# Forget logits of a two-layer hybrid decoder: activations as the stationary operand instead of the weights

## The chip, the cores and the metric

One core of one Trainium2 chip runs the whole program. The metric is the device time of one execution in microseconds (us). Engines are named as in the profile: PE (matrix multiply), PEld (its weight loads), DVE (vector), ACT (scalar and activation), POOL, SP (issues DMAs).

## The reference, cut to what matters

Two layers on 256 tokens of width 1024. Each layer is a SwiGLU block, a mixer and a second SwiGLU block. The mixer projects the normalised activations `h` to queries, keys, values, forget logits (8 columns, one for each head) and the inputs of a recurrent branch. The forget logits enter the attention through a cumulative sum over tokens:

```
h = rms_norm(x, mix_norm[l])
proj = h @ w_in[l] + b_in[l]
q, k, v, f_logit, xr, gr, g_attn, g_rnn = jnp.split(proj, SPLIT_POINTS, axis=-1)
log_f = jax.nn.log_sigmoid(f_logit.astype(jnp.float32))
...
c = jnp.cumsum(log_f, axis=1).transpose(0, 2, 1)
s = jnp.einsum('bhqd,bhkd->bhqk', q_i, k).astype(jnp.float32) * scale
s = s + (c_i[..., :, None] - c[:, :, None, :])
```

## The kernel before, in words

Activations lie transposed: channels on the 128 partitions, in eight chunks, and the 256 tokens along the free axis. The tile `xs` holds for each chunk a rounded part `hi` (columns 0 to 255) and the rest `lo` (256 to 511), both in the type `fp32r`. Each weight block is loaded as `wr`, and split the same way by ACT (`CAST`, the high part) and DVE (`TENSOR_TENSOR`, the rest) into tiles `W` or `R`. A product is three matmuls: high by high, high by low, low by high. One matmul instruction of PE is recorded as a weight load (PEld) of its stationary operand, and a MATMUL over its moving operand. Rows of the order and of the profile name the operands as `out<-moving,stationary`: the forget matmul before the change is `B<-xs,wf`, with the shape `128*16 128x256` in the trace, that is 16 stationary columns and 256 moving ones. The tile `wf2` of the code stands there as `wf`.

The order of instructions on all engines is set while the program is built, by a planner. It keeps a model clock for each engine. The big matrix products are `steps`; everything else is a generator (`forget`, `stats`, `projected`, `qk`, `head`, ...), which yields a time or a condition until which it is put off. When a step is planned, the generators that are due are advanced first, and what they issue goes into the engines' queues there. Each queue is then worked off in this order on the chip, with semaphores between engines.

`mix` starts `forget` at eight steps after the first query projection. `stats` computes the reciprocal norm of each token (`rst`, tokens on partitions) and its copy along the free axis (`rb`); its second pair of matmuls is `B<-S,ones_r`. The weights of the forget logits, 8 columns for each chunk, are split into `wf2`: 8 high columns and 8 low ones side by side.

`forget` before the change: for each chunk, one matmul with the 16 columns of `wf2` stationary and the 256 tokens of `hi` moving, and one with the 8 high columns stationary and `lo` moving. They add up in one PSUM bank, with the 16 logit rows on partitions and tokens along the free axis. The bank is copied by ACT or DVE (`flex`) into the zeroed tile `fpad`, and two PE transposes turn that into tokens on partitions. From there on before and after agree: four small DVE operations make `f` (norm, bias, high plus low part), `log1pexp` makes the log of the sigmoid in about fifteen small DVE operations and an Exp on ACT, three matmuls with `tri` and `ones` make the cumulative sum, DVE copies it into `cpad`, PE transposes `cpad`, and a DMA through DRAM spreads it over the partitions (`cb`), which each `head` needs. In the first layer `decays` runs a second such chain on DVE (`tiny<-prm`, `sp`) behind the first.

Of the kernel before, what the change touches and what calls it, by code (L numbers as in the profile page):

```python
# [23 lines left out]
F32 = mybir.dt.float32  # L24
F32R = mybir.dt.float32r
AF = mybir.ActivationFunctionType
ALU = mybir.AluOpType
# [175 lines left out]
class Trunk:  # L203
# [346 lines left out]
    def setup(self):  # L550
        c = self.const
        self.cpad = c.tile([128, 128], F32, name="cpad")
        self.DVE.memset(self.cpad, 0.0)
        self.fpad = c.tile([128, 256], F32, name="fpad")
        self.POOL.memset(self.fpad, 0.0)
        self.prm_sb = c.tile([128, L, NP_], F32, name="prm")

        self.x0 = c.tile([128, 8 + 2048], F32, name="x")
        self.x = self.x0[:, 8:].rearrange("p (a b) -> p a b", a=8)
        cut = lambda k: slice(8 + 256 * k if k else 0, 264 + 256 * k)  # L560
        load_x = lambda q, k: q.dma_start(out=self.x0[:, cut(k)], in_=self.xT_in[:, cut(k)])
        for k in range(2):
            load_x(self.ACT, k)
        self.load_piece(0, slice(0, W0 // 2))
        self.load_piece(0, slice(W0 // 2, W0))
        self.load_piece(0, slice(W0, 2 * W0))
        for k in range(2, 8):
            load_x(self.SP, k)
            if k < 6:
                self.load_piece(k // 2, slice(k % 2 * W0, k % 2 * W0 + W0))  # L570
        self.ACT.activation(self.t([128, 1], "ss", 4), self.cpad[:, 0:1], AF.Silu)
        warm = self.take(self.banks)
        for _ in range(WARM):
            self.PE.matmul(warm[:, 0:128], self.cpad, self.cpad, start=True, stop=True)
        self.banks.give(warm)

        self.idents = c.tile([128, 256], F32, name="idents")
        self.ident = self.idents[:, 0:128]
        self.POOL.memset(self.idents, 1.0)
        self.POOL.affine_select(out=self.idents, in_=self.idents, compare_op=ALU.is_equal, fill=0.0, base=0,  # L580
                                pattern=[[0, 2], [-1, 128]], channel_multiplier=1)
        self.ones = c.tile([128, 128], F32, name="ones")
        self.POOL.memset(self.ones, 1.0)
        self.ones_r = self.t([128, 192], "ones_r", 1, F32R, self.ops)[:, 16:144]
        self.DVE.tensor_copy(self.ones_r, self.ones)
        self.mhalf = c.tile([128, 8], F32, name="mhalf")
        self.DVE.memset(self.mhalf, -0.5)
        self.xs = self.t([128, 8, 512], "xs", 1, F32R, self.ops)
        self.starts.append((16, self.load_parameters, "bias"))
        self.starts.append((30, self.constants, "bias"))  # L590
# [314 lines left out]


    def forget(self, M):
        pt = self.take(self.banks)
        for k in range(8):

            xs = self.x_rhs(M["phase"], k)
            self.PE.matmul(pt[0:16, 0:256], M["wf2"][:, k], xs[:, 0:256], start=k == 0, stop=False)
            self.PE.matmul(pt[0:8, 0:256], M["wf2"][:, k, 0:8], xs[:, 256:512], start=False, stop=k == 7)
        self.flex(self.fpad[0:16], pt[0:16, 0:256])
        self.banks.give(pt)
        yield self.when(self.fpad, must=lambda: M["phase"] in self.rb, bank=True, queues=())
        pt = self.take(self.banks)
        p3 = self.transpose(pt, self.fpad)
        f = self.t([128, 2, 8], "f", 1)
        for t in range(2):  # L920
            r = self.rms(M["phase"])[:, t:t + 1]
            self.DVE.scalar_tensor_tensor(f[:, t], p3[:, t, 8:16], r, M["bf"], op0=ALU.mult, op1=ALU.add)
            self.DVE.scalar_tensor_tensor(f[:, t], p3[:, t, 0:8], r, f[:, t], op0=ALU.mult, op1=ALU.add)
        self.banks.give(pt)
        yield self.when(f, queues=())
        lp = self.log1pexp(f, [128, 2, 8])
        self.DVE.tensor_scalar(f, f, 0.0, None, op0=ALU.min)
        self.DVE.tensor_sub(f, f, lp)
        if M["l"] == 0:
            self.decays()  # L930
        yield self.when(f, bank=True, queues=())
        pt = self.take(self.banks)
        mm = self.PE.matmul
        mm(pt[:, 0:8], self.tri, f[:, 0], start=True, stop=True)
        mm(pt[:, 8:16], self.ones, f[:, 0], start=True, stop=False)
        mm(pt[:, 8:16], self.tri, f[:, 1], start=False, stop=True)
        self.DVE.tensor_copy(self.cpad[:, 0:16], pt[:, 0:16])
        self.banks.give(pt)
        nc = self.t([128, 16], "nc", 2)
        self.DVE.tensor_scalar(nc, self.cpad[:, 0:16], -1.0, None, op0=ALU.mult)  # L940
        yield self.when(nc, bank=True, queues=())
        pt = self.take(self.banks)
        self.PE.transpose(pt[:, 0:128], self.cpad, self.ident)
        cT = self.t([16, 128], "cT", 1)
        self.DVE.tensor_copy(cT, pt[0:16, 0:128])
        self.banks.give(pt)
        cd = self.dram.tile([16, 128], F32, tag="cd", name="cd", bufs=2)
        yield self.when(cT, queues=())
        self.SP.dma_start(out=cd, in_=cT)
        yield self.when(cd, queues=())  # L950
        M["cb"] = [self.slot([8, 128]) for _ in range(2)]
        for t in range(2):
            self.SP.dma_start(out=M["cb"][t][0][:, 0:1024], in_=bass.AP(tensor=cd.tensor, offset=cd.offset + t * 1024,
                                                                          ap=[[0, 128], [1, 1024]]))
        M["nc"] = nc
# [356 lines left out]
```

## Time and profile before

| | |
|---|---|
| median of 3 runs | 1221.62 us (1221.45 to 1222.02) |
| the profiled execution | 1221.39 us, of which span 1219.7 us |
| PE busy | 1214.3 us, 100% of the span |
| PEld busy | 1187.3 us, 97% |
| DVE busy | 856.6 us, 70% |
| ACT busy | 701.3 us, 57% |
| POOL busy | 39.2 us, 3% |

A timeline row gives the start and length of a group of equal instructions in us, then engine, line, operation, tiles, shapes (for PE the stationary operand as partitions * columns, then the moving one), the count, and in brackets idle time ahead of it with what ended it. [...] All instructions have line 160, the helper that issues them.

### The profile page before, as it was taken

To read this page: it belongs to the slowest core of one execution; us is meant where nothing else is said; L and a number is where in the kernel's file an instruction comes from. 1 tells how busy PE (TensorE), PEld (TensorE's weight loads), DVE (VectorE), ACT (ScalarE), POOL (GpSimd) and SP (SyncE) were. 2 spreads that over 40 slices of the span, in tenths; PEclk is the share of its full clock that TensorE was granted. 3 is DMA by queue.
4 is the path that set the end of the run, shared out by engine and by line. 5 is a ranking of instruction groups with operands and counts; after the bars stand their busy time and mean duration, and the time that the engine had idled before them with its cause. 6 is when DMAs were issued, how large, how long until landed. Compare 5 with 4: busy or idle time off the path is not lost.

```text
span 1219.7 us, 24091 instructions
## 1 busy us (share of the span) xinstructions
PE 1214.3 (100%) x10024; PEld 1187.3 (97%) x10024; DVE 856.6 (70%) x1419; ACT 701.3 (57%) x1231; POOL 39.2 (3%) x48
## 2 busy tenths in 40 slices
PE   9999999999999999999999999999999999999998
PEld 9999998989999999999999999989899999999998
DVE  6775566886869877656677555677876698886742
ACT  6554455789685565444455444465887855654431
POOL 0000000101000000000000000011010000000000
PEclk9999999999999999999999999999999999999999
DMA  7575564543456565545556545646544455565551
GB/s 283 206 252 175 182 234 170 193 179 138 173 171 213 199 248 208 173 173 173 207 208 239 176 149 180 235 145 228 173 142 172 171 207 208 208 224 192 174 191 53
DMA packets 36894, 232.48 MB, mean 191 GB/s; under 512 B 4624, under 2 KB 7088, under 8 KB 10032
## 3 DMA queue, kind: packets, MB, share of 16 engines
q1 hardware_dynamic: 36496, 230.66, 53.8%
q8 instruction: 79, 1.29, 0.4%
q10 hardware_dynamic: 288, 0.27, 0.1%
q14 instruction: 31, 0.25, 0.1%
HBM read 229.85 MB, written 1.06 MB: 189 GB/s over the span
## 4 chain that ended last, share of the span: by engine, by line
PE 98%; ACT 1%; DVE 1%; DMA 0%; issue 0%; ACTq 0%
PE B L160 98%; DVE tiny L160 0%; ACT junk L160 0%; DMA x<-xT 0%; ACT W L160 0%; ACT L160 0%; DVE S L160 0%; ACT xs L160 0%; ACT tiny L160 0%; DVE x L160 0%; DVE sp L160 0%; DVE f L160 0%; DVE sp_neg L160 0%; DVE rq L160 0%; DVE rst L160 0%
## 5 line engine op out<-in xcount | busy, mean ns | idle before, releaser
L160 DVE TENSOR_TENSOR W<-wr,W 128x1024 fp32r<-128x1024 f32 (+2 forms) x316 | 380.3, 1209 | 155.7 <-ACT W L160 153.9
L160 PE MATMUL B<-xs,W 128*128 128x256 f32 x3984 | 472.7, 278 | 0.9 <-ACT W L160 0.9
L160 PEld LDWEIGHTS B<-xs,W 128*128 128x128 f32 x3984 | 462.2, 189 | 2.2 <-ACT W L160 1.2
L160 ACT CAST W<-wr 128x1024 fp32r<-128x1024 f32 (+2 forms) x316 | 323.7, 1034 | 162.5 <-PE B L160 136.4
L160 PE MATMUL B<-R,W 128*128 128x256 f32 x2520 | 291.6, 276 | 0.0
L160 PEld LDWEIGHTS B<-R,W 128*128 128x128 f32 x2520 | 288.3, 188 | 0.0
L160 PE MATMUL B<-xs,R 128*128 128x256 f32 x1776 | 207.5, 276 | 0.0
L160 PEld LDWEIGHTS B<-xs,R 128*128 128x128 f32 x1776 | 204.4, 188 | 0.2
L160 DVE TENSOR_TENSOR R<-wr,R 128x1024 fp32r<-128x1024 f32 x112 | 135.3, 1220 | 35.7 <-ACT R L160 35.7
L160 ACT ACTIVATE S<-S 128x256 f32<-128x256 f32 x88 | 36.1, 418 | 146.2 <-DVE S L160 146.2
L160 PE MATMUL B<-W,xs 128*128 128x512 f32 x492 | 119.2, 393 | 0.0
L160 ACT CAST R<-wr 128x1024 fp32r<-128x1024 f32 x112 | 114.6, 1042 | 0.9 <-DMA wr<-ws 0.9
L160 PEld LDWEIGHTS B<-W,xs 128*128 128x128 f32 x492 | 90.5, 188 | 17.9
L160 PE MATMUL B<-R,R 128*128 128x256 f32 (+1 forms) x808 | 102.8, 280 | 0.0
L160 PEld LDWEIGHTS B<-R,R 128*128 128x128 f32 x808 | 95.2, 188 | 0.0
L160 ACT ACTIVATE xs<-x,prm 128x256 fp32r<-128x256 f32 x40 | 20.1, 508 | 65.6 <-DVE x L160 65.6
L160 POOL TENSOR_TENSOR rst<-rst,mhalf 128x4 f32<-128x4 f32 (+1 forms) x22 | 28.6, 1305 | 888.2 <-DVE rst L160 868.4
L160 DVE TENSOR_TENSOR R<-S,R 128x256 fp32r<-128x256 f32 x88 | 36.5, 422 | 29.2 <-ACT R L160 29.2
L160 DVE TENSOR_TENSOR S<-B,S 128x256 f32<-128x256 f32 x88 | 36.5, 420 | 14.3 <-PE B L160 12.5
L160 ACT CAST R<-S 128x256 fp32r<-128x256 f32 x88 | 34.3, 398 | 13.6 <-DVE S L160 13.6
L160 DVE TENSOR_TENSOR sq<-B,rb 128x256 f32<-128x256 f32 x24 | 10.2, 425 | 43.6 <-PE B L160 43.6
L160 DVE TENSOR_TENSOR S<-B,rb 128x256 f32<-128x256 f32 x88 | 36.1, 418 | 0.1
(126 smaller groups left out, 677.3 us busy)
## 6 DMA issues: line engine op xcount, KB each, us to landing
wr<-ws SPq DMA_DIRECT2D x209, 1024.0 KB, 4.8
wr<-w SPq DMA_DIRECT2D x7, 384.0 KB, 5.4
bias<-b_in SPq DMA_DIRECT2D x8, 256.0 KB, 4.8
R<-wbd SPq DMA_DIRECT2D x4, 512.0 KB, 5.9
R<-cd SPq DMA_DIRECT2D x4, 512.0 KB, 5.9
out<-x SPq DMA_DIRECT2D x8, 128.0 KB, 1.7
x<-xT SPq DMA_DIRECT2D x6, 128.0 KB, 5.4
wr<-w SPq DMA_DIRECT2D x2, 192.0 KB, 3.7
```

Source lines behind the costliest of these rows:

```text
L160: return fn(*args, **kw)
```

## The change

The two operands of the forget matmuls are exchanged. For each half of the tokens (t = 0, 1) and each chunk, 128 tokens of `hi` are stationary and the 16 columns of `wf2` move, and 128 tokens of `lo` are stationary and its 8 high columns move. The result has tokens on partitions already: 16 columns of the bank for each t. `fpad`, its memset, its copy out of PSUM and the two transposes of it are gone, and DVE reads the bank itself. The matmuls are now issued only when `rb` of this phase has been planned, where the transposes were before.

```diff
     def forget(self, M):
+        yield self.when(must=lambda: M["phase"] in self.rb, bank=True, queues=())
         pt = self.take(self.banks)
-        for k in range(8):
-            xs = self.x_rhs(M["phase"], k)
-            self.PE.matmul(pt[0:16, 0:256], M["wf2"][:, k], xs[:, 0:256], start=k == 0, stop=False)
-            self.PE.matmul(pt[0:8, 0:256], M["wf2"][:, k, 0:8], xs[:, 256:512], start=False, stop=k == 7)
-        self.flex(self.fpad[0:16], pt[0:16, 0:256])
-        self.banks.give(pt)
-        yield self.when(self.fpad, must=lambda: M["phase"] in self.rb, bank=True, queues=())
-        pt = self.take(self.banks)
-        p3 = self.transpose(pt, self.fpad)
+        for t in range(2):
+            o, c = pt[:, t * 16:t * 16 + 16], slice(t * 128, (t + 1) * 128)
+            for k in range(8):
+                xs = self.x_rhs(M["phase"], k)
+                self.PE.matmul(o, xs[:, 0:256][:, c], M["wf2"][:, k], start=k == 0, stop=False)
+                self.PE.matmul(o[:, 0:8], xs[:, 256:512][:, c], M["wf2"][:, k, 0:8], start=False, stop=k == 7)
         f = self.t([128, 2, 8], "f", 1)
         for t in range(2):
             r = self.rms(M["phase"])[:, t:t + 1]
-            self.DVE.scalar_tensor_tensor(f[:, t], p3[:, t, 8:16], r, M["bf"], op0=ALU.mult, op1=ALU.add)
-            self.DVE.scalar_tensor_tensor(f[:, t], p3[:, t, 0:8], r, f[:, t], op0=ALU.mult, op1=ALU.add)
+            hi, lo = (pt[:, t * 16 + i:t * 16 + i + 8] for i in (0, 8))
+            self.DVE.scalar_tensor_tensor(f[:, t], hi, r, M["bf"], op0=ALU.mult, op1=ALU.add)
+            self.DVE.scalar_tensor_tensor(f[:, t], lo, r, f[:, t], op0=ALU.mult, op1=ALU.add)
```

Since the planner's clock moves with every instruction, the order around the change moves as well. On PE, in the first layer, this stands in the kernel before (the number behind `_` is a buffer; the last operand of a row is the stationary one; `128x512` matmuls belong to the query and key projections):

```order
L160 MATMUL B_2491<-xs,wf_2257 16x256
L160 MATMUL B_2491<-xs,wf_2257 8x256
L160 MATMUL B_2519<-R_2354,xs 128x512
...
L160 MATMUL B_2519<-W_2415,xs 128x512
L160 MATMUL B_2543<-S_2438,ones_r 128x256 x2
L160 MATMUL B_2554<-idents,fpad 128x128 x2
L160 MATMUL B_2530<-W_2415,xs 128x512
```

And this in the changed kernel, where 16 pairs like the two rows with `wf` follow each other:

```order
L160 MATMUL B_2506<-W_2413,xs 128x512
L160 MATMUL B_2533<-S_2436,ones_r 128x256 x2
L160 MATMUL B_2544<-wf_2255,xs 128x16
L160 MATMUL B_2544<-wf_2255,xs 128x8
...
L160 MATMUL B_2495<-R_2425,xs 128x512
```

The forget matmuls moved behind the second `ones_r` pair, and 32 stand where two transposes stood. Behind them, up to the three matmuls with `tri` and `ones`, PE has 24 matmuls with 512 moving columns, four transposes and 12 matmuls with 256 moving columns, in both layers; before, it had 30, four and 24 behind the transposes of `fpad`.

On DVE, in the first layer, the operations that make `f` stood like this before (`S<-B` are the query rows leaving PSUM, `rst<-ss` their norm, and W and R the low parts of weight blocks):

```order
L160 SCALAR_TENSOR_TENSOR S_2438<-idents,rst,S_2438 128x128 x2
L160 TENSOR_TENSOR W_2516<-wr,W_2515 128x1024
L160 TENSOR_TENSOR R_2527<-R_2489,R_2526 128x1024
L160 SCALAR_TENSOR_TENSOR S_2548<-B_2397,rst,bias 128x512
L160 SCALAR_TENSOR_TENSOR S_2550<-B_2431,rst,bias 128x512
L160 SCALAR_TENSOR_TENSOR f<-B_2554,rst,bf 128x8
...
L160 TENSOR_TENSOR W_2569<-wr,W_2568 128x1024
L160 TENSOR_SCALAR rst<-ss_2578 128x4
L160 SCALAR_TENSOR_TENSOR tiny<-f 128x16
```

They stand like this in the changed kernel:

```order
L160 TENSOR_TENSOR W_2492<-wr,W_2491 128x1024
L160 TENSOR_TENSOR R_2503<-wr,R_2502 128x1024
L160 SCALAR_TENSOR_TENSOR S_2436<-idents,rst,S_2436 128x128 x2
L160 TENSOR_TENSOR R_2518<-R_2487,R_2517 128x1024
L160 SCALAR_TENSOR_TENSOR S_2538<-B_2395,rst,bias 128x512
L160 SCALAR_TENSOR_TENSOR S_2540<-B_2429,rst,bias 128x512
L160 SCALAR_TENSOR_TENSOR f<-B_2544,rst,bf 128x8
...
L160 TENSOR_SCALAR rst<-ss_2582 128x4
L160 TENSOR_TENSOR W_2606<-wr,W_2605 128x1024
L160 SCALAR_TENSOR_TENSOR tiny<-f 128x16
```

One more weight block has been split ahead of `f`, and the same operations follow it. On ACT the eight squares of the query rows (`junk`) moved ahead of the weight cast that stood before them.

The third place is further down on DVE in the first layer, where the cumulative sum leaves PSUM (`COPY cpad`). Before:

```order
L160 SCALAR_TENSOR_TENSOR S_2674<-B_2519,rst,bias 128x512
L160 SCALAR_TENSOR_TENSOR S_2682<-B_2530,rst,bias 128x512
L160 TENSOR_SCALAR R_2711<-mhalf,nb 128x3 x4
L160 TENSOR_TENSOR R_2711<-B_2686,rb 128x256
L160 COPY cpad<-B_2717 128x16
```

And in the changed kernel:

```order
L160 SCALAR_TENSOR_TENSOR S_2690<-B_2495,rst,bias 128x512
L160 SCALAR_TENSOR_TENSOR S_2698<-B_2506,rst,bias 128x512
L160 COPY cpad<-B_2715 128x16
L160 TENSOR_SCALAR nc<-cpad 128x16
L160 TENSOR_SCALAR R_2734<-mhalf,nb 128x3 x4
```

The copy moved ahead of five operations of the recurrent branch.

More of the change, by code (lines that the diff above doesn't have):

```diff
@@ L553, in setup @@
         self.DVE.memset(self.cpad, 0.0)
-        self.fpad = c.tile([128, 256], F32, name="fpad")
-        self.POOL.memset(self.fpad, 0.0)
         self.prm_sb = c.tile([128, L, NP_], F32, name="prm")
```

## The prediction

> **What bounds the kernel now.** I read the page's busy times first, then its chain of work that ended last, then who waited for whom on PE, and then the timeline of PE, at its start and around the forget matmuls.
>
> ```profile
> PE 1214.3 (100%) x10024; PEld 1187.3 (97%) x10024; DVE 856.6 (70%) x1419; ACT 701.3 (57%) x1231; POOL 39.2 (3%) x48
> ...
> PE 98%; ACT 1%; DVE 1%; DMA 0%; issue 0%; ACTq 0%
> ```
>
> ```profile
> 1.12 2.93 PE L160 MATMUL B<-cpad 128*128 128x128 f32 x12 [1.12 <-DVE cpad L160]
> 4.98 6.29 PE L160 MATMUL B<-xs,W 128*128 128x256 f32 x35 [0.93 <-ACT W L160]
> ```
>
> PE is hardly ever short of work: 98% of the chain is its own, and the view of who waited for whom names just these two waits for it, ahead of the warm-up and of the first real matmul. So time goes into the sum of what PE executes, and another engine counts only from the point at which it makes PE wait. What an instruction costs is then its distance to the next start on PE, not its recorded length.
>
> The stretch of the first layer in which the change lies:
>
> ```profile
> 195.85 0.40 PE L160 MATMUL B<-S,ones_r 128*128 128x256 f32 x2
> 196.08 2.91 PE L160 MATMUL B<-W,xs 128*128 128x512 f32 x12
> 198.83 2.01 PE L160 MATMUL B<-xs,wf 128*16 128x256 f32 x16
> 200.68 2.93 PE L160 MATMUL B<-R,xs 128*128 128x512 f32 x12
> ...
> 204.80 0.40 PE L160 MATMUL B<-S,ones_r 128*128 128x256 f32 x2
> 205.04 0.38 PE L160 MATMUL B<-idents,fpad 128*128 128x128 f32 x2
> 205.18 1.64 PE L160 MATMUL B<-W,xs 128*128 128x512 f32 x6
> 206.65 2.91 PE L160 MATMUL B<-R,xs 128*128 128x512 f32 x12
> ...
> 212.60 2.90 PE L160 MATMUL B<-xs,R 128*128 128x256 f32 x24
> 215.35 0.28 PE L160 MATMUL B<-f,tri 128*128 128x8 f32 x2
> 215.48 0.37 PE L160 MATMUL B<-f,ones 128*128 128x8 f32 x2
> ...
> 215.93 2.99 PE L160 MATMUL B<-xs,W 128*128 128x256 f32 x24
> 218.75 0.60 PE L160 MATMUL B<-idents,S 128*128 128x128 f32 x4
> 219.11 1.62 PE L160 MATMUL B<-xs,W 128*128 128x256 f32 x12
> 220.88 0.30 PE L160 MATMUL B<-idents,cpad 128*128 128x128 f32 x1
> 220.93 4.34 PE L160 MATMUL B<-xs,W 128*128 128x256 f32 x36
> ```
>
> From start to start, a matmul with 512 moving columns costs 0.229 us (2.75 for twelve), and one with 256 costs 0.115 (2.75 for 24). And the same places in the second layer:
>
> ```profile
> 803.43 2.01 PE L160 MATMUL B<-xs,wf 128*16 128x256 f32 x16
> 805.27 2.93 PE L160 MATMUL B<-R,xs 128*128 128x512 f32 x12
> ...
> 809.40 0.40 PE L160 MATMUL B<-S,ones_r 128*128 128x256 f32 x2
> ...
> 811.25 2.91 PE L160 MATMUL B<-R,xs 128*128 128x512 f32 x12
> ```
>
> **The change part by part.** *Old matmuls gone.* Sixteen each layer: 198.83 to 200.68 is 1.85 us, 803.43 to 805.27 is 1.84. They cost 0.116 each like any matmul with 256 moving columns; that only 16 or 8 columns were stationary saved nothing. Together -3.69 us.
>
> *Transposes gone.* From 204.80 to 206.65 stand two `ones_r`, two transposes and six wide ones: 1.85 - 0.23 (195.85 to 196.08) - 6 x 0.229 = 0.25 us. The second layer has 1.85 between the same places (809.40 to 811.25). Together -0.50 us.
>
> *New matmuls.* 64 in all, and each has a stationary block of 128 columns of its own, since hi and lo, eight chunks and two token halves make 32 blocks in each layer, and none is used twice. The moving side is 16 or 8 columns. The trace has exactly this form in the cumulative sum: three products of plain f32 with 8 moving columns, two recorded matmuls each. From 215.48 to 215.93 four of them take 0.45 us, 0.1125 each, hardly less than one with 256 columns. What fills it is the load of the stationary block:
>
> ```profile
> L160 PEld LDWEIGHTS B<-xs,wf 128*16 128x16 f32 x16 | 1.5, 94 | 0.5
> ...
> L160 PEld LDWEIGHTS B<-f,tri 128*128 128x128 f32 x8 | 1.2, 190 | 0.0
> ```
>
> 112 more columns make a load 96 ns longer, 0.86 ns a column, or 110 ns for 128. These loads follow each other and are hidden only behind a matmul that streams as long, which 256 columns do and 16 do not. The trace does not show this form with `fp32r` operands, so I bound it. From below 0.108: the six narrow ones take 0.58 us with their edges, and the 24 matmuls behind them 2.82 (to 218.75) instead of 2.75, which is 0.65 for six. From above 0.116: the old forget matmul, in which a load and a longer stream both fit. I take 0.1125, the steady spacing of the nearest shape, since 32 in a row have little edge: 64 x 0.1125 = +7.20 us, between 6.9 and 7.4.
>
> [...]
>
> *The wait at `cpad`.* In the first layer 219.11 to 220.88 is 1.77 us for twelve matmuls worth 1.38, so PE stood about 0.3 us (the rest is slow starts) until DVE had copied the cumulative sum.
>
> ```profile
> 214.47 0.17 DVE L160 TENSOR_TENSOR f<-f,tiny 128x16 f32<-128x16 f32 x1
> ...
> 218.40 1.40 DVE L160 SCALAR_TENSOR_TENSOR S<-B,rst,bias 128x512 f32<-128x512 f32 x2
> 219.71 0.61 DVE L160 TENSOR_SCALAR R<-mhalf,nb 128x3 f32<-128x3 f32 x4
> ...
> 220.56 0.17 DVE L160 COPY cpad<-B 128x16 f32<-128x16 f32 x1
> ```
>
> In the changed order the copy stands right behind the two `S<-B`, so 0.85 us (220.56 - 219.71) earlier after `f`. PE then has 36 matmuls of 0.115 between `tri` and the transpose, 4.1 us, as before. -0.3 us; bounds 0 and -0.4.
>
> *The copy into `fpad` and its memset.* Off PE's path, and ACT and DVE get ahead:
>
> ```profile
> 200.94 0.37 ACT L160 ACTIVATE fpad<-B 16x256 f32<-16x256 f32 x1 [4.06 <-PE B L160]
> ...
> 205.24 0.38 ACT L160 ACTIVATE rb<-B 128x256 f32<-128x256 f32 x1 [1.46 <-PE B L160]
> ...
> 207.57 0.31 ACT L160 ACTIVATE junk<-S 128x128 f32<-128x128 f32 x1
> ...
> 210.04 1.28 ACT L160 ACT_TABLE_LOAD   x1
> 211.34 0.22 ACT L160 ACTIVATE tiny<-tiny 128x16 f32<-128x16 f32 x1
> ```
>
> ACT stood 4.06 us with `fpad` at the head of its queue. Now nothing holds the weight casts there. Worth nothing at the end, since PE did not wait for weights.
>
> *The wait added.* DVE's four `f` operations now stand behind 32 matmuls instead of two transposes. Behind them in DVE's queue are `rst<-ss`, one weight block's low part, and the log chain; the one who waits is PE at `tri`. Let T be the start of the 32. They end at T + 3.6. `f` takes four DVE operations, 1.24 us with the gap behind them:
>
> ```profile
> 206.46 0.22 DVE L160 SCALAR_TENSOR_TENSOR f<-B,rst,bf 128x8 f32<-128x8 f32 x1
> ...
> 207.70 1.23 DVE L160 TENSOR_TENSOR W<-wr,W 128x1024 fp32r<-128x1024 f32 x1 [0.36 <-ACT W L160]
> ```
>
> then the weight block, 1.23, and two small ones, 0.3: T + 6.4 or so. ACT has done its part by then: `rb` starts 0.44 after the start of the `ones_r` pair, which ends at T, so at T + 0.2; the eight squares take 2.47 (207.57 to 210.04), a cast about 1.0, the table 1.28: T + 5.4. From the Exp to the end of `f` it takes 3.3 (211.34 to 214.64), so `f` is ready at T + 9.7. PE reaches `tri` at T + 3.6 + 24 x 0.229 + 4 x 0.13 + 12 x 0.115 = T + 11.0. Hidden by 1.3 us; if that cover were gone, PE would stand for what the chain exceeds it. Weights are not short: the block split behind `f` is first used 133 matmuls behind the 32 in PE's order, at 0.115 or more each over 15 us.
>
> *Sum.* -3.69 - 0.50 + 7.20 - 0.3 = +2.7 us, between +2.3 and +3.2. The profiled execution took 1221.39 us (span 1219.7 and 1.7 around it), so 1224.1. The median of the runs is 0.23 above that execution: 1224.3.
>
> **The rivals.** *A: the loads are hidden further than the row of `tri` shows.* There each product is f32 in two passes over the same block, here every block is new and `fp32r`. For it speaks that PE's first `tri` pair takes 0.13 for two, its loads having been made ahead; against it that the four behind it do not. At that pair's 0.065 each the change would be 64 x 0.065 - 4.2 - 0.3 = -0.3, so 1221.3, no change that can be told. To end faster it would need under 0.032 each ((4.2 + 0.3 - 2.44) / 64), which is loads wholly hidden; then only the stream is left, and 256 more columns cost 0.229 - 0.115 = 0.114 us, so 16 cost 0.007: 0.5 - 4.5 = -4.0, 1217.6. [...]
>
> *B: the clock of PE falls.* The start of the trace shows PE working at half its later rate, at full granted clock:
>
> ```profile
> 6.00:8.00 2.00, 2.00 (x11) 1.00 1.02 368
> 212.60:214.60 2.00, 2.00 (x19) 1.00 0.00 0
> ```
>
> Eleven matmuls with 256 moving columns fall into 2 us at the start, 19 later. In the new block the array streams 16 columns where it streamed 256, for 3.6 us, the longest such stretch in the kernel; the six narrow ones of the cumulative sum, 0.6 us, did not slow what followed. If it fell for as long as the block lasts, 3.6 us at half speed lose 1.8 us in each layer: +3.6 more, 1227.9. [...]
>
> *C: the new wait shows.* If DVE's chain took from the end of the 32 as long as it took from the first `f` before, 214.64 - 206.46 = 8.2 us, it would end at T + 11.8 or 12, and PE would stand 1.0 us at `tri` in each layer: +2.0 on top, 1226.3. It decides from a delay of 1.3 us on. Against it: 3.75 us of the old 8.2 were ACT's squares and table, which now run beside the 32 matmuls for the most part.
>
> *D: each new matmul runs in two passes* as plain f32 does. Then 64 more loads, +7.2: 1231.5. Against it: sixteen `xs,wf` rows for sixteen products in the code.
>
> **How the numbers follow.** About 0.2% is what a measurement of this kernel tells from no change: below 1219.2 is faster, above 1224.06 slower. My forecast, the sum with its own bounds, has 0.62; it runs from 1223.9 to 1224.8, and two thirds of it lie above 1224.06. A has 0.16, of which 0.04 for loads hidden wholly. B has 0.08, C 0.10, D 0.04. Slower: 0.42 + 0.08 + 0.10 + 0.04 = 0.64; same: 0.20 + 0.12 = 0.32; faster: 0.04. The range reaches from 1222.5, on the way to A, to C's price, 1226.3. It leaves out the outer half of A's 0.12, the wholly hidden loads, D, and the half of B in which the low rate lasts so long, 0.18 together.
>
> **What would show it.** The rows `B<-wf,xs` 32 to a layer, start to start 3.6 us from the first to the row behind; their loads about 190 ns; none of `fpad`; no wait at `tri`, and none at `cpad` in the first layer; PE's busy time and span both longer by near 3 us. Rows nearer to 2.6 us for 32 mean A; wide matmuls behind them at 0.2 apiece mean B; idle time at `tri` means C; 64 rows in a layer mean D. Wrong it would be above all if two `fp32r` loads can be held ahead of the matmul, which no row here shows.

## The result, and the profile after

The changed kernel takes 1227.89 us in the median of four runs (1224.9, 1227.45, 1228.33, 1228.88), beside 1221.53 for the kernel before, measured with it: a ratio of 1.005, 95% interval 1.0038 to 1.0063. That is slower by 6.4 us, where 1224.3 was forecast with a range up to 1226.3. The direction was right, the time lies outside the range, and it lies at the price of rival B, 1227.9. One run of all those below, of the kernel with more warm-up, took 1521.51 us at a mean granted clock of 0.753 and is left out of the range given there.

The profiled execution is the fastest of the four, 1224.9 us (span 1223.2). The changed block in PE's timeline, first layer and then second (columns: start, time from the first start to the last end, engine, line, operation, output and operands, shapes, count; an end is modelled, so durations are read from start to start):

```profile
195.00 0.40 PE L160 MATMUL B<-S,ones_r 128*128 128x256 f32 x2
...
203.41 0.40 PE L160 MATMUL B<-S,ones_r 128*128 128x256 f32 x2
203.65 3.63 PE L160 MATMUL B<-wf,xs 128*128 128x16 f32 x32
207.14 1.63 PE L160 MATMUL B<-R,xs 128*128 128x512 f32 x6
208.61 0.60 PE L160 MATMUL B<-idents,S 128*128 128x128 f32 x4
...
213.16 1.54 PE L160 MATMUL B<-xs,R 128*128 128x256 f32 x12
214.55 0.28 PE L160 MATMUL B<-f,tri 128*128 128x8 f32 x2
...
216.59 2.89 PE L160 MATMUL B<-xs,W 128*128 128x256 f32 x24
219.31 0.27 PE L160 MATMUL B<-idents,cpad 128*128 128x128 f32 x1
...
809.24 3.63 PE L160 MATMUL B<-wf,xs 128*128 128x16 f32 x32
812.73 2.33 PE L160 MATMUL B<-R,xs 128*128 128x512 f32 x6
814.85 1.05 PE L160 MATMUL B<-idents,S 128*128 128x128 f32 x4
815.56 2.22 PE L160 MATMUL B<-R,xs 128*128 128x512 f32 x6
817.62 2.91 PE L160 MATMUL B<-W,xs 128*128 128x512 f32 x12
```

The block is 3.49 us long in both layers (207.14 - 203.65 and 812.73 - 809.24), 0.109 for each matmul. What follows it differs: six matmuls with 512 columns take 1.47 us in the first layer (to the next row, at 208.61) and 2.12 in the second. PE's windows tell why. They are laid on the grid on which the clock changes: its records in this trace stand at 4.45 us (full), 813.40 (half), 816.82 (full) and 1223.00 (half, with PE's work done), and the two long stretches between them, 808.959 and 406.186 us, are 237 and 119 times the short one, 3.413 (columns: window, its length, PE's busy time, in brackets the matmuls that touch it, granted clock, DMA share, GB/s):

```profile
202.42:205.83 3.41, 3.41 (x29) 1.00 0.07 25
205.83:209.24 3.41, 3.41 (x25) 1.00 0.92 266
...
809.99:813.40 3.41, 3.41 (x29) 1.00 0.70 105
813.40:816.82 3.42, 3.42 (x12) 0.50 0.72 276
816.82:820.23 3.41, 3.41 (x16) 1.00 0.01 2
```

Behind the second layer's block the granted clock is 0.50 for 3.413 us and full again. By the clock that loses 1.71 us, half of it, as an estimate; by the rows, the 16 matmuls behind the block take 4.89 us there (812.73 to 817.62) and 3.30 in the first layer (207.14 to 210.44), 1.59 more. The block fills 2.74 of the 3.41 us of the window ahead of the fall (809.99 to 812.73), a share of 0.80; in the first layer the two windows that it touches are filled to 0.64 and 0.38, and the clock holds. By the page's first and fourth parts nothing has happened:

```profile
PE 1217.4 (100%) x10052; PEld 1190.7 (97%) x10052; DVE 855.5 (70%) x1415; ACT 702.0 (57%) x1233; POOL 41.8 (3%) x47
...
PE 98%; ACT 1%; DMA 0%; DVE 0%; issue 0%; SPq 0%; ACTq 0%
```

PE is busy throughout, and the page's clock row is a 9 in each of its slices, which are 30 us long. A fall of 3.4 us is seen only in windows of its own length, and in the run's mean granted clock: 0.999 in the profiled run, 0.997 and twice 0.996 in the others. The mean of one fall is 1 - 1.71/1223 = 0.9986, of two 0.9972, of three 0.9958. So the median run has lost what two falls cost, or more. Every run of the kernel before whose clock is on record stood at 1.000.

### The profile page after: what moved, and what is told of

The parts are those of the page before. It is cut to its first block, busy times and chain, and to the rows that moved or that the text cites. A ratio compares the mean times of both kernels' runs of the same rounds, so it can differ in the third digit from the quotient of the medians.

```text
span 1223.2 us, 24142 instructions
## 1 busy us (share of the span) xinstructions
PE 1217.4 (100%) x10052; PEld 1190.7 (97%) x10052; DVE 855.5 (70%) x1415; ACT 702.0 (57%) x1233; POOL 41.8 (3%) x47
## 4 chain that ended last, share of the span: by engine, by line
PE 98%; ACT 1%; DMA 0%; DVE 0%; issue 0%; SPq 0%; ACTq 0%
PE B L160 98%; ACT R L160 0%; DMA wr<-w 0%; ACT W L160 0%; ACT L160 0%; DVE W L160 0%; ACT xs L160 0%; DVE x L160 0%; SPq L160 0%; ACT sq L160 0%; ACT acc L160 0%; ACTq L160 0%
## 5 line engine op out<-in xcount | busy, mean ns | idle before, releaser
L160 DVE TENSOR_TENSOR W<-wr,W 128x1024 fp32r<-128x1024 f32 (+2 forms) x310 | 372.6, 1208 | 161.8 <-ACT W L160 159.5
L160 PE MATMUL B<-xs,W 128*128 128x256 f32 x3888 | 459.6, 278 | 1.6 <-ACT W L160 1.3
L160 PEld LDWEIGHTS B<-xs,W 128*128 128x128 f32 x3888 | 449.1, 188 | 3.2 <-ACT W L160 1.8
L160 ACT CAST W<-wr 128x1024 fp32r<-128x1024 f32 (+2 forms) x310 | 317.2, 1034 | 174.2 <-PE B L160 147.1
L160 PE MATMUL B<-xs,R 128*128 128x256 f32 x1872 | 220.5, 276 | 0.0
L160 PEld LDWEIGHTS B<-xs,R 128*128 128x128 f32 x1872 | 216.1, 188 | 0.3
L160 DVE TENSOR_TENSOR R<-wr,R 128x1024 fp32r<-128x1024 f32 x118 | 142.6, 1219 | 36.0 <-ACT R L160 36.0
L160 ACT CAST R<-wr 128x1024 fp32r<-128x1024 f32 x118 | 121.0, 1042 | 0.7 <-DMA wr<-ws 0.7
L160 PE MATMUL B<-W,xs 128*128 128x512 f32 x468 | 111.6, 392 | 0.0
L160 POOL TENSOR_TENSOR rst<-rst,mhalf 128x4 f32<-128x4 f32 (+1 forms) x22 | 33.0, 1504 | 897.7 <-DVE rst L160 897.7
```

The costliest lines, as they stand in the source:

```text
L160: return fn(*args, **kw)
```

## The experiments

The first four kernels set the theory that the block lets the clock fall (B) against the theories that the new order makes PE wait, that something else about the new matmuls brings the clock down, or that chance had made the runs long. The kernel before had medians of 1221.07 to 1221.35 us beside the experiments.

**The changed kernel again** (no edit).

> The changed kernel once more, to see how its time scatters. Theory (clock): the 32 narrow matmuls of a layer leave most of a 3.4 us window with hardly any streaming, PE's granted clock then falls to half for one 3.413 us window, and whether it falls depends on where the window's edge lies against the block. Each fall costs 1.7 us on top of the +2.7 us of the sum: single runs between 1223.5 and 1229 us, the longer ones with the lower mean granted clock (0.999 for one fall, 0.997 for two). Rival (waits): the reordered queues make PE wait; then every run is near 1227.9 us whatever its clock.

Measured: 1228.56 us (1224.87 to 1229.63), ratio 1.0054 (1.0041 to 1.0067). This time the profiled run has a clock of 0.997, and two falls. Its timeline, and its windows on its own grid:

```profile
205.02 3.88 PE L160 MATMUL B<-wf,xs 128*128 128x16 f32 x32
...
812.25 3.63 PE L160 MATMUL B<-wf,xs 128*128 128x16 f32 x32
```

```profile
204.84:208.25 3.41, 3.41 (x33) 1.00 0.20 54
208.25:211.67 3.42, 3.42 (x11) 0.50 0.88 303
211.67:215.08 3.41, 3.41 (x18) 1.00 0.07 29
...
812.41:815.82 3.41, 3.41 (x34) 1.00 0.30 68
815.82:819.24 3.42, 3.42 (x12) 0.50 0.82 299
```

The two falls are 607.57 us apart, which is 178 times 3.413, and the two blocks 607.23 (205.02 to 812.25): the falls keep to the grid and not to the kernel. The block begins 0.18 us after a grid line in the first layer (204.84, 205.02) and just before one in the second, so that it fills 0.95 and 0.98 of a window, and both are followed by a fall. In the two profiles of this kernel the number of falls, one and two, goes with where the grid lies when the block comes. All nine runs of this kernel in the two sets lie below 1.000; none had no fall.

**A pause between the halves.** The planner is asked to put 2 us of other work between t = 0 and t = 1.

```diff
         for t in range(2):
+            if t:
+                yield self.when(after=2.0, queues=())
```

> The 32 narrow matmuls of a layer in two lots of 16 with twelve matmuls of 512 moving columns between, so at most 1.8 us of any 3.4 us are narrow. Clock theory: granted clock 1.000 in every run, and the bare sum is left: 1224.2 us (1223.3 to 1225.0). Rival (waits): the same work waits on the same queues, 1227 to 1228 us. Rival (the clock falls for another reason than this block): clock below 1.000 in some runs, 1226 or more.

Measured: 1232.24 us (1231.83 to 1232.6), ratio 1.0089 (1.0075 to 1.0102), clock 0.997 in every run. The fall behind the block is gone, but the kernel is slower still. The planner wrote a new order for all that follows, and in it `tri` comes later:

```profile
219.91 0.28 PE L160 MATMUL B<-f,tri 128*128 128x8 f32 x2
```

In the second layer PE waits near 1000 us for products of the recurrent branch; that the later `tri` is the reason is likely and not shown. The waits (engine, line, what it waited for, us in total, times, longest), and the clock, which falls behind that idle time:

```profile
PE B L160 <- DVE R L160: 3.6, 1, 3.6
PE B L160 <- ACT R L160: 1.7, 1, 1.7
```

```profile
995.00:998.50 3.50, 1.18 (x9) 1.00 0.11 44
998.50:1001.90 3.40, 0.39 (x2) 0.50 0.78 289
1001.90:1005.30 3.40, 3.40 (x17) 0.50 0.35 96
1005.30:1008.70 3.40, 3.40 (x31) 1.00 0.57 236
```

So 5.3 us of waiting and 6.8 us at half speed where none stood. The expectation missed because the edit changed the order; this run says nothing on the price of the block.

**256 moving columns for 16.** Each of the 32 matmuls streams the 16 columns of the weights 16 times over (a stride of zero) and writes 256 columns, of which the kernel reads the first 16. The loads stay what they were.

```diff
+        wide = lambda k: bass.AP(tensor=M["wf2"].tensor, offset=M["wf2"][:, k].offset, ap=[M["wf2"].ap[0], [0, 16], [1, 16]])
...
-                self.PE.matmul(o, xs[:, 0:256][:, c], M["wf2"][:, k], start=k == 0, stop=False)
-                self.PE.matmul(o[:, 0:8], xs[:, 256:512][:, c], M["wf2"][:, k, 0:8], start=False, stop=k == 7)
+                self.PE.matmul(o, xs[:, 0:256][:, c], wide(k), start=k == 0, stop=False)
+                self.PE.matmul(o, xs[:, 256:512][:, c], wide(k), start=False, stop=k == 7)
```

> The same 32 matmuls with the same stationary blocks and as many loads in one lot, but each streams 256 moving columns (the 16 weight columns read 16 times over). Clock theory, by streamed columns: granted clock 1.000 in every run, 32 matmuls cost 3.7 us a layer instead of 3.5: 1224.6 us (1223.8 to 1225.5). Rival (the stationary activations or the place in the order do it): clock below 1.000 and near 1228 us as before.

Measured: 1234.42 us (1233.24 to 1235.78), ratio 1.0107 (1.0093 to 1.0121). Again no fall at the block, and again a new order, with waits of 2.7 and 2.5 us for the recurrent branch and 1.5 for `S`, and a fall at 1003 to 1010 us behind them. It missed for the same reason, and decides nothing on the block.

**Twice the block.** All 32 matmuls are issued twice in each layer.

```diff
-        for t in range(2):
+        for t in (0, 1, 0, 1):
```

> The narrow block issued twice in a row, 64 matmuls in a layer, 7.2 us at full clock (the second pass writes the same values again). Clock theory: at least one whole window lies inside the block, so the clock falls in both layers of every run, part of the block itself runs at half rate, and the wide matmuls behind it too: 1224.3 + 7.2 + 8 to 12 = 1239 to 1243 us, mean granted clock near 0.99. Rival (waits): 1227.9 + 7.2 = 1235 us at clock 1.000.

Measured: 1242.68 us (1241.0 to 1243.35), ratio 1.0168 (1.0154 to 1.0182), clock 0.990 to 0.991, as B has it. The 64 more matmuls account for 64 x 0.109 = 7.0 of the 14.1 us between this and the second set of the changed kernel (1228.56). The rest is mostly the clock, here in the first layer (the order around the block moved here too, with one wait of 0.3 us for `S`):

```profile
204.71:208.12 3.41, 3.41 (x33) 1.00 0.12 43
208.12:211.54 3.42, 3.42 (x19) 0.50 0.81 310
211.54:214.95 3.41, 3.41 (x18) 0.50 0.10 36
214.95:218.36 3.41, 3.41 (x11) 0.50 0.01 2
218.36:221.77 3.41, 3.41 (x21) 1.00 0.00 0
```

Three windows at half speed follow three windows that the block fills to 0.93 and more: each costs the next one. In the second layer it is four:

```profile
829.35:832.76 3.41, 3.41 (x11) 0.50 0.00 0
832.76:836.17 3.41, 3.41 (x13) 0.50 0.00 0
```

```profile
830.13 2.91 PE L160 MATMUL B<-R,xs 128*128 128x512 f32 x6
```

The fourth follows a window of which the block fills only 0.23 (829.35 to 830.13). Wide matmuls stream through the other 0.77, but at half speed, and the clock stays down for one window more.

In the kernels that follow, the order of everything else is held fixed. The planner's clock is charged for the matmuls of the changed kernel (`charge`), and what is really issued goes past the planner (`mm`), so that no other instruction moves. In the traces of all seven of these kernels every other matmul, and every instruction of DVE, ACT and POOL, follows in the order of the changed kernel.

```diff
+        mm, charge = self.PE.engine.matmul, lambda *a: self.clock.issue("PE", "matmul", a, {})
...
-                self.PE.matmul(o, xs[:, 0:256][:, c], M["wf2"][:, k], start=k == 0, stop=False)
-                self.PE.matmul(o[:, 0:8], xs[:, 256:512][:, c], M["wf2"][:, k, 0:8], start=False, stop=k == 7)
+                charge(o, xs[:, 0:256][:, c], M["wf2"][:, k])
+                charge(o[:, 0:8], xs[:, 256:512][:, c], M["wf2"][:, k, 0:8])
```

**256, 128 and 64 columns, order held.** `mm` streams `wide(k)` as above, with 16, 8 or 4 repeats. At 0.114 us for 256 columns (0.229 for 512 less 0.115 for 256) 128 columns stream, as an estimate, for half of the 0.109 us that a matmul of the block takes, and 64 for a quarter.

> As pad256 (32 matmuls, same loads, 256 columns streamed instead of 16 or 8), but the planner is charged as for the narrow ones, so every queue stands exactly as in the changed kernel. Clock theory by streamed columns: granted clock 1.000 in every run, and the bare sum: 1224.4 us (1223.5 to 1225.3). Rival (order): the extra time of the changed kernel comes from its new order; then 1228 us and more. Rival (stationary activations): clock below 1.000 and 1228 us.

> [...] With 64 columns the clock fell in three of five runs, with 256 in none of six. If it goes by the streamed share of a window, and half suffices: granted clock 1.000 in every run, 1224.1 us (1223.5 to 1224.9). If not: some runs at 0.999 to 0.997 and 1.7 us more for each fall.

> [...] If the clock goes by the streamed share and its bound lies above a quarter, it falls as in the changed kernel: 1226 to 1229.5 us, clock 0.999 to 0.996. If any stream that follows each load keeps it up: 1224.3 us at 1.000.

Measured: 256 columns take 1224.92 us (1224.38 to 1225.32), ratio 1.0031 (1.0019 to 1.0042), clock 1.000 in all six runs. 128 columns take 1224.16 (1223.2 to 1224.98), ratio 1.0025 (1.0016 to 1.0035), 1.000 in all ten. 64 columns take 1224.9 (1224.04 to 1227.89), ratio 1.0037 (1.0024 to 1.005): two of five runs at 1.000 with 1224.04 and 1224.15, the others at 0.998, 0.997 and 0.997. With 256 columns the block, the first row here, is longer than a window and no longer followed by anything:

```profile
205.00:208.90 3.90, 3.90 (x35) 1.00 0.26 73
208.90:212.30 3.40, 3.40 (x19) 1.00 0.75 297
```

The same loads in the same order, with more columns behind each, are some 3 to 4 us *faster* than with 16 (1224.92 and 1224.16 beside 1227.89 and 1228.56). So it is the thin stream and not the loads, the wait or the order that costs the second half of the loss. The changed kernel itself did not run beside these; but the kernel with 64 columns, in the same set as that with 256, lost its clock in three of five runs, and the one with 24 matmuls in a row (below), in the same set as that with 128, too, so the chip on which a set ran is not the difference. In the profile of the 128-column kernel the block fills a window to 0.96, and the clock holds; with 64 columns it held at 0.55 and fell at 0.89.

**A short block, in two ways.** First, 12 matmuls with 480 columns, whose results nobody reads, between the two halves of 16:

```diff
+            for k in range(12 if t == 0 else 0):
+                xs = self.x_rhs(M["phase"], k % 8)
+                mm(pt[:, 32:512], xs[:, 0:128], xs[:, 0:480], start=True, stop=True)
```

> The narrow block kept, but twelve idle wide matmuls (480 columns, into a spare part of the bank) stand between its two halves; all queues as in the changed kernel. It costs 2 x 12 x 0.215 = 5.2 us of PE. Clock theory: no window is more than half narrow, granted clock 1.000 in every run: 1224.2 + 5.2 = 1229.4 us (1228.6 to 1230.4). Rival: 16 narrow in a row suffice, clock below 1.000: 1231 to 1233 us.

Measured: 1229.49 us (1229.14 to 1229.62), ratio 1.0067 (1.0053 to 1.008), clock 1.000 in all. The fill takes 2.68 us in each layer in the trace, so 5.4 of the 8.4 us are the fill and 3.0 are the change with its clock unharmed. Of a window the halves fill 0.50 at most:

```profile
204.12:207.53 3.41, 3.41 (x26) 1.00 0.28 35
207.53:210.94 3.41, 3.41 (x25) 1.00 0.98 289
```

Second, to find the bound, the same 12 behind the first 24 of the 32, a stretch of 2.6 us, which can fill 0.78 of a window at most:

```diff
+                if (t, k) == (1, 3):
+                    for i in range(12):
+                        mm(pt[:, 32:512], self.xs[:, i % 8, 0:128], self.xs[:, i % 8, 0:480], start=False, stop=False)
```

> 24 narrow matmuls, twelve idle wide ones (480 columns), then the other 8; all queues as in the changed kernel. At most 0.78 of a window is narrow. The profiles so far show no fall behind a window that was 0.64 narrow and one behind 0.80. Bound above 0.78: granted clock 1.000, 1229.4 us. Bound between: falls in some runs, 1231.2 us each.

Measured: 1231.33 us (1228.42 to 1232.75), ratio 1.0077 (1.0064 to 1.009). Two runs at 1.000 take 1228.42 and 1228.43, three at 0.997 to 0.998 take 1231.33 to 1232.75. (The first two lie 1 us below the kernel with 16 and 16; in the profiled one, 1228.42, the second `ones_r` pair starts at 203.31, and at 204.44 in the other kernel's profile: that is the start, ahead of any edit.) The profiled run, whose windows the narrow matmuls fill to 0.57, has no fall there; that the other three runs fell is read from their mean clock:

```profile
202.08:205.49 3.41, 3.41 (x28) 1.00 0.09 36
205.49:208.91 3.42, 3.42 (x22) 1.00 0.94 196
```

**Less of the block.** One kernel issues only the products with the high parts of the activations, 16 to a layer, so its logits lack the low parts; the other issues 2 of the 32, for the first chunk alone.

```diff
+                mm(o, xs[:, 0:256][:, c], M["wf2"][:, k], start=k == 0, stop=k == 7)
```

```diff
+                if k == 0:
+                    mm(o, xs[:, 0:256][:, c], M["wf2"][:, k], start=True, stop=True)
```

> Only the 16 narrow matmuls of a layer with the high parts of the activations are left (the logits lack the low parts), one lot of 1.8 us, all queues as in the changed kernel. Clock theory: granted clock 1.000. Price of a narrow matmul 0.109: 1224.2 - 32 x 0.109 = 1220.7 us (1220.2 to 1221.3), so half the block with no fall is no slower than the kernel before. Rival (order): 1228.5 - 3.5 = 1225 us.

> Of the 32 narrow matmuls of a layer only two are left (one for each token half; the logits lack the other seven chunks and the low parts), all queues as in the changed kernel. Clock theory: granted clock 1.000 and the bare sum less 60 x 0.1125 = 6.75: 1217.5 us (1216.7 to 1218.3), so that 60 narrow matmuls are worth over 10 us of the changed kernel's median. Rival (order): the waits stay, 1228.5 - 6.75 = 1221.7 us.

Measured: with 16 1221.26 us (1220.39 to 1222.42), ratio 1.0002 (0.9993 to 1.001), clock 1.000 in all eleven runs, inside the range of B's theory and below the 1225 of the rival. Its block is 1.71 us long, half of the other, 0.107 each:

```profile
205.13 1.85 PE L916 MATMUL B<-wf,xs 128*128 128x16 f32 x16
206.84 1.63 PE L160 MATMUL B<-R,xs 128*128 128x512 f32 x6
```

With two it takes 1220.04 us (1219.38 to 1221.29), ratio 0.9991 (0.9982 to 0.9999), at 1.000; 1217.5 was expected, so 2.5 us of what the block costs did not come back. The timeline and the waits show where they went:

```profile
203.76 0.28 PE L917 MATMUL B<-wf,xs 128*128 128x16 f32 x2
...
212.44 0.36 PE L160 MATMUL B<-f,tri 128*128 128x8 f32 x2 [0.98 <-DVE tiny L160]
```

```profile
PE B L160 <- DVE rst L160: 1.0, 1, 1.0
PE B L160 <- DVE tiny L160: 1.0, 1, 1.0
```

PE now stands about 1 us at `tri` in each layer, and 0.3 at `cpad` (its transpose starts 3.00 us after the first of the 24 matmuls ahead of it, 2.72 in the changed kernel), 2.2 us in all: the block had been the cover of DVE's `f` chain. Here rival C exists, at a block of 0.3 us.

**The start, in the kernel before.** Full clock comes at 9.34 us in the profile of before and at 4.45 in that of the changed kernel (the first record of the clock in each trace), and the `ones_r` pair of the first layer stands at 195.85 in the one and at 195.00 in the other, though ahead of it the two differ on PE, DVE, ACT and POOL only by the memset of `fpad`, on POOL at 0.8 us. Three more products that warm PE up, not charged to the planner, were added to the kernel before:

```diff
+        for _ in range(3):
+            self.PE.engine.matmul(warm[:, 0:128], self.cpad, self.cpad, start=True, stop=True)
```

> The kernel before with three more warm-up products (nine instead of six), so that PE has no gap between the warm-up and its first real matmul; the planner is charged for six and all queues stand as before. Clock theory: PE reaches full rate one window after its first busy one, by 7.9 us at the latest instead of 9 to 10 us in most profiles: 0.3 to 1.5 us faster than before, 1220.3 us. Rival: the start is bound by the transfers, 1221.1 us, no change.

Measured: 1220.61 us (1220.27 to 1220.86), ratio 0.9995 (0.9986 to 1.0004), which can't be told from no change. In its profile the full clock comes at 5.48 us, and its runs scatter less than those of before (1220.37 to 1222.24). One profile each does not show that the start is the whole of that scatter. In the profile of before the window from 2.52 to 5.93 us, in which PE is busy for 2.48 of 3.41, is followed by one at half rate, and that from 5.93 to 9.34, busy throughout, by one at the full rate.

## Why the prediction was wrong, point by point

- **Old matmuls and transposes gone, new matmuls in:** right. The new ones are 0.109 apart where 0.1125 was taken, inside the bounds; 6.98 us for 64. With 4.19 removed that makes +2.8, or +2.5 with the wait at `cpad` gone, and the recorded loads, 192 ns, are as forecast. The change with its clock at 1.000 measures +2.96 (128 columns), +3.0 (two runs with 64 columns) and +3.0 (fill taken off); the sum said +2.7. The half us between +2.5 and +3.0 is not placed. Rivals A and D are refuted by the same 0.109 and by 32 rows to a layer.
- **The wait at `cpad`:** gone as forecast. DVE's copy is done 1.2 us ahead of PE's transpose at 219.31:

```profile
212.65 0.17 DVE L160 TENSOR_TENSOR f<-f,tiny 128x16 f32<-128x16 f32 x1
...
217.91 0.16 DVE L160 COPY cpad<-B 128x16 f32<-128x16 f32 x1
```

- **The wait added, rival C:** hidden, as forecast. `f` is ready at 212.82, PE reaches `tri` at 214.55: 1.7 us to spare where 1.3 was forecast, and no idle time at the `tri` row. The kernel with two matmuls to a layer shows that the cover was the block itself.
- **Rival B, the failed step.** The sum priced every matmul behind the block at full speed and put the clock at nothing; B, which had a term for it, got a chance of 0.08, and the range stopped at 1226.3, below B's 1227.9. In its place the profiles show windows that the block fills to 0.80, 0.95 and 0.98 followed by one at half the clock, which costs 1.71 us by the clock and 1.59 by the rows, and the runs show that the median lost 3.4 us in this way (6.36 less the 2.96 of the change with its clock at 1.000). The argument against B in the prediction was that the six narrow matmuls of the cumulative sum, 0.6 us, "did not slow what followed". They could not: 0.6 us is 0.18 of a window of 3.41, and the clock still held at 0.64. The block is 3.49 us, as long as a whole window. The row told nothing on the case at hand, and a chance near even, with a range up to B's price and beyond, would have followed from that. That B's 1227.9 and the median meet to 0.01 us is luck: the nine runs lie between 1224.87 and 1229.63. The half speed lasted one window (3.413 us) per fall and not "as long as the block lasts", 3.6, and falls come two to a run in the median by the grid's position, not one in each layer for certain.
- **The start, read wrongly.** The prediction took the start for half the later rate "at full granted clock". By the rows it was the half clock itself. The first record of the clock stands at 9.34 us; for the time ahead of it the column says 1.00 without a record, and matmuls with 256 columns run at about half the rate up to just there:

```profile
5.93:9.34 3.41, 3.41 (x18) 1.00 1.02 381
9.34:12.75 3.41, 3.41 (x32) 1.00 1.05 389
```

- **Left open:** the four runs with a clock of 0.996 have lost some three windows by that mean, and none of them was profiled, so where the third falls is not shown. The mean is no exact count either: in the profile of the changed kernel run again, the last 0.78 us of the span, in which PE has no work left, stand at 0.50 too. The one wait that the profile of the changed kernel has and that of before has not, 0.3 us for a weight cast, is no doing of the new order. It lies at the start, where the order on PE is still that of before:

```profile
6.36 4.83 PE L160 MATMUL B<-xs,W 128*128 128x256 f32 x36 [0.33 <-ACT W L160]
```

No variant that makes the whole logits from the exchanged operands beat the kernel before: with the clock held, the change still costs 3 us, since 64 loads of 0.109 replace matmuls worth 4.2.

## What to carry to other kernels

Exchanging operands so that the activations are stationary trades streaming for one load per 128 tokens and chunk: count 0.11 us each, and then ask how much the array streams in that stretch, since here a PE that was busy with loads, for 3.41 of 3.41 us, did not keep its clock. A stretch of 16 such matmuls, 1.7 us, held the clock in all sixteen runs that had no longer one; a stretch of 24, 2.6 us, lost it in three of five. So keep it short, break it with wide work that is due anyway, or let each matmul stream 128 columns instead of 16, which took 3.53 us for the block here beside 3.49. And when an experiment changes what a planner is charged for, hold the order fixed: two of the kernels here that did not, those with the pause and with 256 columns, came out 8 and 10 us above what the edit alone was worth, more than the effect that they were to measure.

## What the runs showed of the hardware

- PE's clock went with what the array streamed and not with how long PE was busy. Ahead of the fall in the profile of the changed kernel PE is busy for 3.41 of 3.41 us (809.99 to 813.40), 2.74 of them the block; with as many loads and 256 or 128 columns streamed behind each, all sixteen runs stood at 1.000. The windows at full speed go with one bound, worked out from the rows as an estimate: at 0.114 us for 256 columns, a matmul with 16 or 8 columns streams 5% of its 0.109 us, with 64 columns 26%, with 128 columns 52%. The share of the window in which the array streams is then 0.39 in the fullest window of narrow matmuls that held (0.36 + 0.64 x 0.05) and 0.54 with 128 columns, and it is 0.34 (0.11 + 0.89 x 0.26, 64 columns), 0.24 (0.20 + 0.80 x 0.05) and less where the clock fell. Ahead of the fall in the kernel with the pause nine matmuls with 256 columns touch the 3.5 us, 0.29 of it at most.
- At half speed the rows agree with the same bound only if columns are counted and not time. In the second layer of the doubled block 0.77 of the window from 829.35 us streams, and the clock stays down; at half rate that is what 0.39 of a window holds at full speed. In its first layer 0.82 streams (215.56 to 218.36), 0.41 in columns, and the clock comes back. Counted so the bound lies at about 0.39 in these runs, as near as the estimate goes. The start of the program, with its plain f32 products, is left out of this.
- A fall lasted one window, 3.413 us in the trace of the changed kernel, and PE then ran at half the rate: around the doubled block 33 matmuls touch a window at full speed and 19 and 18 the next two at half, and six matmuls with 512 columns took 2.71 us in the fall of the kernel run again (208.76 to 211.47) beside 1.47 at the full clock. Around the doubled block the half speed went on for three windows in one layer (10.24 us) and four in the other (13.65); that it ends when a window holds enough columns is the estimate above. One fall cost 1.59 us by the rows, 1.71 by the clock, in this kernel, which PE bounds.
- The grid lay differently from run to run: it has a line 1.23 us ahead of the first layer's block in the one profile of the changed kernel (202.42, 203.65) and 0.18 in the other. So one program has several times: the profiled run with one fall took 1224.9 us, that with two 1228.01.
